# A GLA encoder layer on one core: second-part operands stored by pairs of tiles, half of their blocks kept on chip, and another order of the gate and value products

## The chip, the cores and the metric

The kernel runs on one core of one Trainium2 chip, as one program. The metric is the device time of one execution in microseconds (us). A core has five engines that run their own instruction streams in order: TensorE (PE, matmuls, with a separate weight-load row PEld), VectorE (DVE), ScalarE (ACT), GpSimd (POOL) and SyncE (SP). Here SP only issues DMA transfers. ACT issues some too, between its own instructions.

## The reference, cut to what matters

One layer of an encoder on a sequence of 2048 rows of 1024 numbers in float32: a gated-linear-attention (GLA) mixer, a residual sum, a norm, a convolutional feed-forward part with 2 x 2816 columns up and 1024 down, a second residual sum, and a last norm.

```python
def conv_ffn(h, w_up, conv_w, conv_b, w_down):
    u = causal_dwconv(h @ w_up, conv_w, conv_b)   # three taps along the sequence
    g, val = jnp.split(u, 2, axis=-1)
    return (jax.nn.silu(g) * val) @ w_down

# the layer
h = rmsnorm(x, mix_norm_w)
x = x + gla_mixer(h, w_in, w_gate2, b_gate, norm_w, w_out)
h = rmsnorm(x, ffn_norm_w)
x = x + conv_ffn(h, w_up, conv_w, conv_b, w_down)
return rmsnorm(x, final_norm_w)
```

The change touches the way from the second `rmsnorm` to the products `h @ w_up`, and the order of those products.

## The kernel before, in words

**Products.** Float32 accuracy is made from two float32r numbers, a high part (a cast on ACT, L184) and a low part (a subtraction on DVE, L185); `split` makes both. A product is three matmuls (`mm3p`, L177, L178, L179: high by low, low by high, high by high). Each of the big matrix products is cut into 2 x 2 blocks and made by seven block products p1 to p7 in place of eight (a Strassen-Winograd scheme); their operands are blocks or sums of blocks. p1, p6, p7 and p4 add up in one PSUM bank, p5 and p3 in a second, and p2 has a third.

**Passes.** R, A and B are the projections into the mixer and the scan. Pass Y multiplies by the output projection. When a tile of 128 rows of `x1 = x + y` is complete, `x1_done` (L741) stores it and normalises it (ACT, L747), and `blocks` (L750) transposes it on PE (L756) into two blocks `hb2` of 128 x 512 and stores each to the DRAM scratch `h2f` (L761). There are 16 tiles, so 32 blocks.

**The second-part operands.** For each pair of tiles, `prep_h2` (L764 to L814) loads blocks from `h2f` again (`h2r`, L772), forms the sums that p5, p7, p6 and p4 need (DVE), splits the seven operands into `h2p` (L184, L185), and stores each to the DRAM scratch `hd` with two DMAs of 256 KB (L778). The rows of `hd` are for one half, high or low, of one operand for four pairs, so that one such DMA writes runs of 128 numbers, 512 bytes. `spread` (L816) gives each of these steps a due time on a clock that counts the PE work emitted so far: the first four pairs (sequence half s = 0) during pass Y from Y0 on, a step every Y1 us; the other four pairs (s = 1) during the gate/value products of s = 0, from U0 on, a step every U1 us. In pass Y `h2p` has three buffers, later one.

**Gate and value products, `phase_u(s)`** (L998 to L1147), for each half s of the sequence, 1024 rows. `load_op` (L833) brings the operand of one product on chip with two DMAs of 1 MB, on ACT's queue for s = 0 and on SP's for s = 1. Then come 11 groups g of two column blocks f. A group has 14 jobs (seven products for two blocks), each of 12 matmuls of 128x512. The order of the products is `OPS`: p1, p5, p6, p2, p7, p4, p3. The two raw weight tiles of a block, `ur`, are loaded on SP (L1007) into four buffers; the jobs' weight operands are prepared five jobs ahead (`prep`, L1010): the sums on POOL (L1017, L1020, L1023, and L1026 for p3) into `us` or in place, then the split. The results:
- PSUM bank `ua` collects p1, p6, p7, p4. ACT copies it out as c1, c2, c3 after p1, p6, p7 (`copied`, L1039) and after p4 into the value tile `u` (L1139). The next product into the bank waits for the copy.
- Bank `uc` collects p5 and p3; bank `ub` holds p2.
- `new_u` (L1042) takes one of **three** buffers of tag `u` for the gate (i = 0) or the value (i = 1) of a block and copies two halo columns into it on POOL (L1045). At p2 the gate tile is taken (filled at L1128), at p7 the value tile (filled at L1135, which reads bank `uc`), at p4 the value tile is complete and `conv(1, f)` runs (L1055 on ACT, twice L1057 on DVE), at p3 the gate tile is complete (L1145), `conv(0, f)` runs, and `gated(f)` forms the operand of the down projection; seven operands of 256 KB a group are stored to `ad` by SP (L1068, L1071, L1072, L1084), four of them after sums on POOL (L1078 to L1082).

**Down projection** (L1150 to the end): seven products for two halves, with `ad` and `w_down` as operands.

**What sets the order.** The code emits work in the order above, and a scheduler with a model of the engines puts each engine's instructions in a final order, which the engines keep. DMAs of a core go to eight lanes in turn, and a DMA on a lane is issued only when the DMA before it on that lane has landed: the ninth waits for the first. Where a tile's buffers are used up, the first instruction that writes the next tile waits for the last reader of the oldest.

Of the kernel before, what the change touches and what calls it, by code (L numbers as in the profile page):

```python
# [16 lines left out]
P = 128  # L17
# [3 lines left out]
def f32(ap):  # L21
    return ap.bitcast(F32)
# [3 lines left out]
def hybrid_kernel(  # L26
# [45 lines left out]
    Y0, Y1, U0, U1 = 9.0, 3.6, 20.0, 12.0  # L72
# [13 lines left out]
    OPS = ("p1", "p5", "p6", "p2", "p7", "p4", "p3")  # L86
    PORD = ("p1", "p5", "p6", "p7", "p4", "p2", "p3")
# [642 lines left out]
    def y_open():  # L730
        need(f"scan1_{NTT - 1}", f"scan1_{NTT - 2}")
        sp["bctx"].close()
        sp["actx"].close()
        yp["p"] = p = yp["ctx"].enter_context(tc.tile_pool(name="yp", bufs=1, reuse_waits="tile"))
        spread(range(PAIRS), Y0, Y1, p,
               lambda name: p.tile([P, 512], F32, tag="h2r", name=name, bufs=4),
               lambda name: p.tile([P, 2, 512], F32R, tag="h2p", name=name, bufs=3))
# [12 lines left out]
    def blocks(tt, rws):  # L750

        for k in range(2):
            pt = aux_ps(f"pt_d{tt}_{k}")
            for j in range(HK):
                kt = HK * k + j
                nc.tensor.transpose(pt[:, j * P:(j + 1) * P], rws[:, kt * P:(kt + 1) * P], ident)  # L756
            t = yp["p"].tile([P, 512], F32, tag="hb2", name=f"hb2_{tt}_{k}", bufs=4)
            for j in range(HK):
                kt = HK * k + j
                nc.scalar.activation(t[:, j * P:(j + 1) * P], pt[:, j * P:(j + 1) * P], AF.Identity, scale=nw2[:, kt:kt + 1])  # L760
            nc.sync.dma_start(h2f[tt][k], t)  # L761
        ready.add(f"h2f{tt}")

    def prep_h2(jj, pool, raw, pair):  # L764

        s, j = divmod(jj, PAIRS)
        ts = {}

        def load(n, c, k):
# [10 lines left out]
        sub = nc.vector.tensor_sub  # L780

        def first():
            need(f"h2f{2 * jj}", f"h2f{2 * jj + 1}")
            for n, (c, k) in enumerate(((0, 0), (1, 0), (1, 1))):
                load(n, c, k)

        def p1():
            put("p1", 0)

        def p5():  # L790
            sub(ts[0], ts[1], ts[0])
            put("p5", 0)

        def p7():
            sub(ts[1], ts[2], ts[1])
            put("p7", 1)

        def p3():
            load(1, 0, 1)
            put("p3", 2)  # L800

        def p6():
            sub(ts[0], ts[2], ts[0])
            put("p6", 0)

        def p2():
            put("p2", 1)

        def p4():
            sub(ts[1], ts[1], ts[0])  # L810
            put("p4", 1)
            ready.add(f"h2p{jj}")

        return [first, p1, p5, p7, p3, p6, p2, p4]  # L814
# [18 lines left out]
    def load_op(s, o):  # L833

        t = uh.tile([P, KT, 512], F32R, tag=o, name=f"h_{s}_{o}", bufs=1)
        for i in range(2):
            (nc.scalar if s == 0 else nc.sync).dma_start(f32(t[:, i * HK:(i + 1) * HK, :]), hd[s, o, i])
        hop[o] = (t[:, :HK, :], t[:, HK:, :])
# [159 lines left out]
    def phase_u(s):  # L998
# [11 lines left out]
        def prep(k):  # L1010
# [4 lines left out]
            if o == "p5":  # L1015
                src = sums[f] = out_tile(f"us_{s}_{f}")
                add(src, a21, a22)  # L1017
            elif o == "p6":
                src = sums[f]
                sub(src, src, a11)  # L1020
            elif o == "p7":
                src = a21
                sub(src, a11, a21)  # L1023
            elif o == "p3":
                src = sums.pop(f)
                sub(src, a12, src)  # L1026
            else:
                src = {"p1": a11, "p2": a12, "p4": a22}[o]
# [5 lines left out]
            split(hl[0], hl[1], src)  # L1034
            wops[o, f] = hl
# [54 lines left out]
        for k, (g, o, f) in enumerate(jobs):  # L1090
            if o == "p1" and f == 2 * g and g + 1 < NQ:
                load(g + 1)
            if s == 0 and k == 6:
# [6 lines left out]
                spread(range(PAIRS, 2 * PAIRS), U0, U1, wx_, row_tile,  # L1100
# [11 lines left out]
            pairs = [((wh[:, kt * P:(kt + 1) * P], wl[:, kt * P:(kt + 1) * P]), (hop[o][0][:, kt, :], hop[o][1][:, kt, :])) for kt in range(HK)]  # L1112
# [116 lines left out]
    def d_early(o):  # L1229
# [3 lines left out]
        elif o == "p2":  # L1233
# [147 lines left out]
```

## Time and profile before

| | us |
|---|---|
| median of 3 runs | 2328.84 |
| lowest and highest run | 2320.21, 2340.29 |
| the profiled execution, its own time | 2328.23 |
| span of its trace, first to last instruction | 2326.5 |

The mean granted TensorE clock of the profiled execution is 0.980 of full speed. The trace begins with pass R; pass Y runs from about 750 us to 965 us, the products of s = 0 from about 965 to 1455, those of s = 1 to about 1900, and the down projection to the end. A table by such windows is the way to read this profile, because the stages have different limits. In a row of a waits table, "PE uc L177 <- DVE u L1135" reads: PE's matmul on line 177 into a bank `uc` was idle until DVE's instruction on line 1135 that writes a tile `u`; then the sum in us, the number of times and the longest. In a timeline row the start, the duration, the engine and line, output and inputs; in square brackets the idle time ahead of the instruction and what ended it. "SPq" and "ACTq" are DMA issues of the two engines; a row with x3 is three in a row, from the first issue to the end of the last.

### The profile page before, as it was taken

How to read it: one execution, taken by the hardware profiler on the slowest of the kernel's cores; microseconds unless marked ns; L12 is line 12 of the kernel's file. 1: busy time of each engine (PE TensorE's matmuls, PEld its weight loads, DVE VectorE, ACT ScalarE, POOL GpSimd, SP SyncE). 2: the span in 40 equal slices, each digit the busy share in tenths (PEclk: the TensorE clock that was granted, in tenths of full speed). 3: DMA queues.
4: the chain of work that ended last, by engine and by line, in shares of the span. 5: the costliest groups of instructions: out<-in, count | busy, mean ns of one | idle time of the engine just before them, and what ended most of it. 6: DMA issues, size and time to landing. Idle time of an engine off the chain costs nothing. (4 is left out here: it accounts for less than half of the span.)

```text
span 2326.5 us, 28993 instructions
## 1 busy us (share of the span) xinstructions
PE 2152.4 (93%) x9948; PEld 1746.6 (75%) x9948; DVE 1605.4 (69%) x2175; ACT 1115.9 (48%) x2020; POOL 702.0 (30%) x602
## 2 busy tenths in 40 slices
PE   5999999989997988688898999999999999999998
PEld 4888778877886766566776777877777778888887
DVE  7755787788778555377776777777676786656554
ACT  4554655565555664444444444445444554223243
POOL 1000111111110000245454555464555543134200
PEclk9999999999999999899999999999999999999999
DMA  6545684478556999954444236633323268554443
GB/s 218 191 159 187 203 278 122 124 232 289 166 155 228 304 312 326 350 154 131 138 138 145 77 114 223 223 102 99 106 79 119 75 217 307 180 178 160 135 163 118
DMA packets 344115, 420.14 MB, mean 181 GB/s; under 512 B 22798, under 2 KB 216510, under 8 KB 340384
## 3 DMA queue, kind: packets, MB, share of 16 engines
q1 hardware_dynamic: 313900, 360.35, 47.4%
q10 hardware_dynamic: 30068, 57.95, 7.3%
q8 instruction: 78, 1.28, 0.2%
q14 instruction: 69, 0.57, 0.1%
HBM read 270.89 MB, written 147.32 MB: 180 GB/s over the span
## 5 line engine op out<-in xcount | busy, mean ns | idle before, releaser
L177 PE MATMUL ua<-h_p,uw_p 128*128 128x512 f32 x704 | 283.0, 402 | 24.7 <-ACT c L1039 24.7
L178 PE MATMUL ua<-h_p,uw_p 128*128 128x512 f32 x704 | 281.2, 399 | 0.0
L179 PE MATMUL ua<-h_p,uw_p 128*128 128x512 f32 x704 | 280.8, 399 | 0.0
L1057 DVE SCALAR_TENSOR_TENSOR t<-u,cw,t 128x1024 f32<-128x1024 f32 x176 | 244.6, 1418 | 21.9 <-issue 8.2
L178 PE MATMUL pd_p<-dw_p,da 128*128 128x512 f32 x616 | 239.8, 389 | 0.3 <-DVE da L185 0.3
L177 PE MATMUL pd_p<-dw_p,da 128*128 128x512 f32 x616 | 239.6, 389 | 0.0
L179 PE MATMUL pd_p<-dw_p,da 128*128 128x512 f32 x616 | 239.6, 389 | 0.0
L185 DVE TENSOR_TENSOR da<-da_p,da 128x512 fp32r<-128x512 f32 x154 | 128.9, 891 | 102.9 <-ACT da L184 102.7
L185 DVE TENSOR_TENSOR uw_p<-us,uw_p 128x512 fp32r<-128x512 f32 x132 | 138.4, 1049 | 72.5 <-ACT uw_p L184 71.9
L184 ACT CAST da<-da_p 128x512 fp32r<-128x512 f32 x154 | 85.4, 619 | 204.7 <-PE pd_p L179 154.5
L177 PEld LDWEIGHTS ua<-h_p,uw_p 128*128 128x128 f32 x704 | 135.7, 193 | 58.2 <-ACT c L1039 27.7
L185 DVE TENSOR_TENSOR uw_p<-ur,uw_p 128x512 fp32r<-128x512 f32 x176 | 137.9, 794 | 54.0 <-ACT uw_p L184 52.1
L177 PE MATMUL uc<-h_p,uw_p 128*128 128x512 f32 x352 | 141.6, 402 | 35.1 <-DVE u L1135 35.0
L178 PEld LDWEIGHTS ua<-h_p,uw_p 128*128 128x128 f32 x704 | 135.9, 193 | 30.7 <-DVE uw_p L185 0.4
L179 PEld LDWEIGHTS ua<-h_p,uw_p 128*128 128x128 f32 x704 | 135.5, 193 | 30.8
L184 ACT CAST uw_p<-ur 128x512 fp32r<-128x512 f32 x176 | 107.9, 620 | 72.5 <-PE ub L179 43.8
L178 PE MATMUL uc<-h_p,uw_p 128*128 128x512 f32 x352 | 139.2, 395 | 0.0
L179 PE MATMUL uc<-h_p,uw_p 128*128 128x512 f32 x352 | 139.2, 395 | 0.0
L1039 ACT COPY c<-ua 128x512 f32<-128x512 f32 x132 | 77.1, 584 | 127.2 <-PE ua L179 127.0
L1017 POOL TENSOR_TENSOR us<-ur 128x512 f32<-128x512 f32 x44 | 66.8, 1518 | 234.1 <-DMA ur<-in_ffn_w_up_dram 229.0
L178 PEld LDWEIGHTS pd_p<-dw_p,da 128*128 128x128 f32 x616 | 115.6, 188 | 24.6 <-DVE da L185 0.7
L179 PEld LDWEIGHTS pd_p<-dw_p,da 128*128 128x128 f32 x616 | 115.6, 188 | 24.1
(250 smaller groups left out, 5503.1 us busy)
## 6 DMA issues: line engine op xcount, KB each, us to landing
ur<-in_ffn_w_up_dram SPq DMA_DIRECT2D x84, 512.0 KB, 4.0
da_p<-ad_p SPq DMA_DIRECT2D x154, 256.0 KB, 4.0
hd_p<-h2p_p SPq DMA_DIRECT2D x112, 256.0 KB, 3.9
ad_p<-as_p SPq DMA_DIRECT2D x88, 256.0 KB, 2.0
ad_p<-t SPq DMA_DIRECT2D x66, 256.0 KB, 2.9
x<-in_x_dram SPq DMA_DIRECT2D x32, 512.0 KB, 5.1
ch<-in_ffn_w_down_dram SPq DMA_DIRECT2D x61, 256.0 KB, 4.9
hr_A_p<-h1d_p SPq DMA_DIRECT2D x56, 256.0 KB, 2.8
```

What stands on the lines that cost most here:

```text
L177: nc.tensor.matmul(ps_ap, ah, bl, start=(first and i == 0), stop=False, **kw)
L178: nc.tensor.matmul(ps_ap, al, bh, start=False, stop=False, **kw)
L179: nc.tensor.matmul(ps_ap, ah, bh, start=False, stop=(last and i == len(pairs) - 1), **kw)
L184: nc.scalar.copy(hi, src)
L185: nc.vector.tensor_sub(lo, src, f32(hi))
L1017: add(src, a21, a22)
L1039: nc.scalar.copy(t, pa)
L1057: nc.vector.scalar_tensor_tensor(t, u[:, k:k + TS], cw[:, k, c:c + 1], t, op0=ALU.mult, op1=ALU.add)
```

## The change

1. The blocks of the first eight tiles (s = 0) stay on chip: `hb2` gets ten buffers, and their 16 stores to `h2f` and 16 loads from it go. The blocks of the other eight tiles still go through `h2f`, which has one scratch array per tile now (tag `hb3`, two buffers in place of four).
2. `hd` is kept by pairs: one array [128, 2, 512] per product and pair, with the high and the low part side by side. One store of 512 KB takes the place of two of 256 KB, and it is issued at the next step (`held`), not right behind its split. `load_op` has four DMAs of 512 KB in place of two of 1 MB, and the matmul's moving operand is a view of four runs of 128 numbers, one for each pair.
3. `spread` is one chain of steps that waits until the blocks of a pair are there. Y0, Y1 go from 9.0, 3.6 to 3.0, 2.8, and U1 from 12.0 to 11.0.
4. `OPS` becomes p1, p5, p6, p7, p4, p2, p3, and with it the order of the jobs and of the operand loads. An early load for the down projection hangs on p7 in place of p2.
5. The sum for p3 (POOL) is made right behind the split for p6, and not when p3's weights are prepared.

```diff
-    Y0, Y1, U0, U1 = 9.0, 3.6, 20.0, 12.0
+    Y0, Y1, U0, U1 = 3.0, 2.8, 20.0, 11.0
...
-    OPS = ("p1", "p5", "p6", "p2", "p7", "p4", "p3")
-    PORD = ("p1", "p5", "p6", "p7", "p4", "p2", "p3")
+    OPS = PORD = ("p1", "p5", "p6", "p7", "p4", "p2", "p3")
...
-    h2f = [[scratch([P, 512], f"h2f_{t}_{k}") for k in range(2)] for t in range(NTT)]
+    h2f = {t: scratch([P, 2, 512], f"h2f_{t}") for t in range(TT, NTT)}
...
-    hd = {(s, o, i): scratch([P, HK, 512], f"hd_{s}_{o}_{i}") for s in range(NS) for o in OPS for i in range(2)}
+    hd = {(s, o, j): scratch([P, 2, 512], f"hd_{s}_{o}_{j}") for s in range(NS) for o in OPS for j in range(PAIRS)}
...
-            t = yp["p"].tile([P, 512], F32, tag="hb2", name=f"hb2_{tt}_{k}", bufs=4)
+            t = hb2_tile(f"hb2_{tt}_{k}", tt < TT)
...
-            nc.sync.dma_start(h2f[tt][k], t)
+            if tt < TT:
+                h2[tt, k] = t
+            else:
+                nc.sync.dma_start(h2f[tt][:, k, :], t)
         ready.add(f"h2f{tt}")
 
-    def prep_h2(jj, pool, raw, pair):
+    def hb2_tile(name, kept):
+        return yp["p"].tile([P, 512], F32, tag="hb2" if kept else "hb3", name=name, bufs=10 if kept else 2)
+
+    def prep_h2(jj, raw, pair):
...
         def load(n, c, k):
+            if s == 0:
+                ts[n] = h2.pop((2 * jj + c, k))
+                return
             if n not in ts:
                 ts[n] = raw(f"h2r_{jj}_{n}")
-            nc.sync.dma_start(ts[n], h2f[2 * jj + c][k])
-
-        def put(o, n):
+            nc.sync.dma_start(ts[n], h2f[2 * jj + c][:, k, :])
+
+        def store():
+            while held:
+                o, hl = held.pop()
+                nc.sync.dma_start(hd[s, o, j], f32(hl))
+
+        def step(o, n, x=None, y=None, then=None):
+            store()
+            if x is not None:
+                nc.vector.tensor_sub(ts[n], ts[x], ts[y])
+            if then is not None:
+                then()
             hl = pair(f"h2p_{jj}_{o}")
             split(hl[:, 0, :], hl[:, 1, :], ts[n])
-            for i in range(2):
-                nc.sync.dma_start(hd[s, o, i][:, :, j * P:(j + 1) * P], f32(hl[:, i, :]).rearrange("p (a b) -> p a b", b=P))
+            held.append((o, hl))
...
     def spread(pairs, t0, dt, *how):
-        for n, jj in enumerate(pairs):
+
+        chain_ = []
+        for jj in pairs:
             for i, fn in enumerate(prep_h2(jj, *how)):
-                later_do(t0 + dt * (7 * n + max(0, i - 1)) - (2.0 if i == 0 else 0.0), fn)
+                chain_.append((fn, dt if 0 < i < 8 else 2.0, {f"h2f{2 * jj}", f"h2f{2 * jj + 1}"}))
+
+        def go():
+            fn, us, what = chain_[0]
+            if not ready.issuperset(what):
+                later_do(2.0, go)
+                return
+            chain_.pop(0)
+            fn()
+            if chain_:
+                later_do(us, go)
+
+        later_do(t0, go)
...
-        t = uh.tile([P, KT, 512], F32R, tag=o, name=f"h_{s}_{o}", bufs=1)
-        for i in range(2):
-            (nc.scalar if s == 0 else nc.sync).dma_start(f32(t[:, i * HK:(i + 1) * HK, :]), hd[s, o, i])
-        hop[o] = (t[:, :HK, :], t[:, HK:, :])
+        t = uh.tile([P, 2, PAIRS, 512], F32R, tag=o, name=f"h_{s}_{o}", bufs=1)
+        for j in range(PAIRS):
+            (nc.scalar if s == 0 else nc.sync).dma_start(f32(t[:, :, j, :]), hd[s, o, j])
+        hop[o] = tuple(t[:, i].rearrange("p j (k c) -> p k j c", c=P) for i in range(2))
...
             elif o == "p3":
                 src = sums.pop(f)
-                sub(src, a12, src)
...
             split(hl[0], hl[1], src)
+            if o == "p6":
+                sub(src, a12, src)
             wops[o, f] = hl
...
-        elif o == "p2":
+        elif o == "p7":
             d_load(4)
```

**Where instructions stand now: the `u` tiles (POOL).** In the rows, `u_0_c` is the tile of sequence half 0 and column block c: 4 and 5 are the gates of a group, 26 and 27 its values, 6 and 28 those of the next group. L1045 (L1055 in the change) takes a tile, L1053 (L1063) saves its halo when the first half of `conv` has come. Before:

```order
L1053 COPY halo_500<-u_0_26_10581 128x2
L1020 TENSOR_TENSOR us_0_6_10625<-us_0_6_10625,ur_0_6_10400 128x512
L1020 TENSOR_TENSOR us_0_7_10654<-us_0_7_10654,ur_0_7_10404 128x512
L1026 TENSOR_TENSOR us_0_6_10625<-ur_0_6_10400,us_0_6_10625 128x512
L1045 COPY u_0_27_10601<-halo_500 128x2
L1053 COPY halo_500<-u_0_27_10601 128x2
```

And in the changed kernel:

```order
L1063 COPY halo_504<-u_0_26_10478 128x2
L1063 COPY halo_504<-u_0_27_10502 128x2
L1029 TENSOR_TENSOR us_0_6_10566<-us_0_6_10566,ur_0_6_10342 128x512
L1055 COPY u_0_5_10589<-halo_504 128x2
L1055 COPY u_0_28_10798<-halo_504 128x2
L1029 TENSOR_TENSOR us_0_7_10592<-us_0_7_10592,ur_0_7_10346 128x512
L1063 COPY halo_504<-u_0_4_10563 128x2
L1044 TENSOR_TENSOR us_0_6_10566<-ur_0_6_10342,us_0_6_10566 128x512
```

The fourth tile of the group, the one that can be taken only when the first is free, was the second block's value (27, for p7) and is now the second block's gate (5, for p2). PE's order in a group is now p1, p5, p6, p7 for both blocks, 19 of the 24 matmuls of p2, p4 for both blocks, the last five of p2, p3; before it was p1, p5, p6, p2, p7, p4, p3, with the first block's p1 of the next group begun inside p3.

**The stores of the s = 1 operands in the group (SP).** These are SP's rows in the first groups of s = 0; `ad` and `as` belong to the gated operands, `ur` are raw weight tiles, `hd` the operand stores of `h2p`. Before:

```order
L1084 DMA ad_0_p3_0_404<-as_0_0_p3_10075 128x512
L1084 DMA ad_0_p7_0_382<-as_0_0_p7_10078 128x512
L1007 DMA ur_0_5_10085<-in_ffn_w_up_dram 128x8x128
L1007 DMA ur_0_27_10087<-in_ffn_w_up_dram 128x8x128
L778 DMA hd_1_p2_1_331<-h2p_4_p2_10549 512x1x128
L772 DMA h2r_5_2_10759<-h2f_11_1_277 128x512
L778 DMA hd_1_p4_0_334<-h2p_4_p4_10643 512x1x128
```

And now:

```order
L1094 DMA ad_0_p7_0_375<-as_0_0_p7_10020 128x512
L1016 DMA ur_0_4_10023<-in_ffn_w_up_dram 128x8x128
L1016 DMA ur_0_26_10025<-in_ffn_w_up_dram 128x8x128
L1016 DMA ur_0_5_10027<-in_ffn_w_up_dram 128x8x128
L1016 DMA ur_0_27_10029<-in_ffn_w_up_dram 128x8x128
L785 DMA hd_1_p6_0_322<-h2p_4_p6_10415 128x1024
L785 DMA hd_1_p2_0_334<-h2p_4_p2_10491 128x1024
L780 DMA h2r_5_2_10721<-h2f_11_257 128x512
```

A store of `hd` still stands behind the gated stores of the group and behind raw weight loads, four in a row now where there were two there and two earlier.

**The operand loads of s = 1 (SP).** At the end of s = 0, `h_1_o` is the operand of product o, and the group before it is group 10. Before:

```order
L1084 DMA ad_0_p7_10_392<-as_0_10_p7_13233 128x512
L1007 DMA ur_1_3_13248<-in_ffn_w_up_dram 128x8x128
L1007 DMA ur_1_25_13250<-in_ffn_w_up_dram 128x8x128
L837 DMA h_1_p4_13472<-hd_1_p4_0_334 128x2048
L837 DMA h_1_p4_13472<-hd_1_p4_1_335 128x2048
L837 DMA h_1_p3_13517<-hd_1_p3_0_336 128x2048
```

And now:

```order
L1094 DMA ad_0_p7_10_385<-as_0_10_p7_13151 128x512
L1016 DMA ur_1_2_13162<-in_ffn_w_up_dram 128x8x128
L1016 DMA ur_1_24_13164<-in_ffn_w_up_dram 128x8x128
L1016 DMA ur_1_3_13166<-in_ffn_w_up_dram 128x8x128
L1016 DMA ur_1_25_13168<-in_ffn_w_up_dram 128x8x128
L846 DMA h_1_p4_13357<-hd_1_p4_3_333 128x2x512
L846 DMA h_1_p2_13402<-hd_1_p2_0_334 128x2x512
L846 DMA h_1_p2_13402<-hd_1_p2_1_335 128x2x512
```

Behind the last gated store of group 10 there stood the operands of p4 and p3, and now stand the last quarter of p4, the whole of p2 and that of p3.

More of the change, by code (lines that the diff above doesn't have):

```diff
@@ L734, in y_open @@
         yp["p"] = p = yp["ctx"].enter_context(tc.tile_pool(name="yp", bufs=1, reuse_waits="tile"))
-        spread(range(PAIRS), Y0, Y1, p,
-               lambda name: p.tile([P, 512], F32, tag="h2r", name=name, bufs=4),
+        spread(range(PAIRS), Y0, Y1, None,
                lambda name: p.tile([P, 2, 512], F32R, tag="h2p", name=name, bufs=3))
@@ L790, in p5, with last @@
[L790 to L811, printed above, removed]
-            ready.add(f"h2p{jj}")
-        return [first, p1, p5, p7, p3, p6, p2, p4]
+        def last():
+            store()
+            ready.add(f"h2p{jj}")
@@ L1111, in phase_u @@
             wh, wl = wops.pop((o, f))
[L1112 removed]
+            pairs = [((wh[:, kt * P:(kt + 1) * P], wl[:, kt * P:(kt + 1) * P]), (hop[o][0][:, kt], hop[o][1][:, kt])) for kt in range(HK)]
             if o == "p1":
```

12 lines of the change are left out of this document (7 added, 5 removed).

## The prediction

> **What bounds the kernel now.** I read the busy shares first, then the span in windows by stage, then what PE waited for in each stage, then the chain that ended last inside one stage, and last the timelines of the queues at the places that these name.
>
> ```profile
> PE 2152.4 (93%) x9948; PEld 1746.6 (75%) x9948; DVE 1605.4 (69%) x2175; ACT 1115.9 (48%) x2020; POOL 702.0 (30%) x602
> 750.00:930.00 180.00, 160.75 (x726) 123.69 (x725) 100.32 (x167) 103.26 (x228) 11.73 (x17) 1.00 0.92 309
> 930.00:965.00 35.00, 17.20 (x50) 11.77 (x50) 5.74 (x10) 8.83 (x18) 3.59 (x4) 0.75 1.04 407
> 1005.00:1345.00 340.00, 302.30 (x1234) 241.94 (x1235) 251.60 (x264) 155.75 (x232) 169.74 (x149) 0.94 0.44 130
> 1455.00:1900.00 445.00, 427.07 (x1848) 345.36 (x1847) 329.05 (x339) 215.85 (x317) 230.38 (x173) 1.00 0.41 128
> ```
>
> The window rows give from:to, length, then the busy time (and count) of PE, PEld, DVE, ACT and POOL, the granted clock, the DMA share and GB/s. The kernel is bound by PE nearly everywhere: 93% busy. So a change that removes no matmul can win only where PE idles or runs at a lower clock. Three places show that. Pass Y has 19 us idle in 180 with the DMA engines 92% busy. The change from Y to the products is half idle (17.2 of 35) with the clock at 0.75 and the DMA engines full. And the products of s = 0 take longer than those of s = 1: a group is 14 x 12 = 168 matmuls, so the s = 0 window holds 1234/168 = 7.3 groups, 46 us each, and the s = 1 window 11 groups, 40.5 each. At the full-speed spacing of 0.23 us, which the rows from 1243.63 further down show, a group would take 38 to 39 us. The down projection (417.88 of 426 busy) has nothing to give, and the passes before Y are in the same order before and after.
>
> ```profile
> PE uc L177 <- DVE u L1135: 35.0, 20, 3.0
> PE ua L177 <- ACT c L1039: 24.4, 6, 4.9
> PE uc L177 <- DVE u L1135: 14.0, 7, 3.0
> PE uc L177 <- DVE u L1135: 21.1, 13, 2.3
> ```
>
> The first row is of the whole span, the second and third of 965 to 1345, the fourth of 1345 to 1900. So two waits make the products slow: p3 of the second block waits for L1135 to free bank `uc` in nearly every group, and p4 waits for the ACT copy c3 in s = 0 alone, some 4 us each time. The chain inside one group of s = 0 says what is behind both (start, length, what):
>
> ```profile
> 1220.33 1.11 DVE uw_p L185
> ...
> 1222.48 5.53 DMA hd_p<-h2p_p
> ...
> 1228.60 0.59 ACT c L1039
> 1229.23 0.79 PE ua L177
> ...
> 1234.69 0.59 ACT u L1139
> ...
> 1235.80 1.15 ACT t L1055
> 1236.97 2.01 DVE t L1057
> ...
> 1242.47 0.61 DVE u L1135
> 1243.13 0.50 PE uc L177
> 1243.63 0.23 PE uc L178
> 1243.86 0.23 PE uc L179
> ```
>
> Read from the end: p3 (1243.13) waits for L1135 of the second block, which writes the group's fourth `u` tile; its buffer comes free only through L1139, L1055 and both L1057 of the first block, that is after p4. In the first half of the piece p4 (1229.23) waits for c3 (1228.60), and that follows the DMA of an operand store, which SP could issue only at 1222.48, behind a raw weight load, which waited for the split (1220.33) that freed its buffer. Why ACT waits for a store, and why SP is late, the two queues show:
>
> ```profile
> 1228.08 0.62 ACT L184 CAST h2p_p<-h2r 128x512 fp32r<-128x512 f32 x1 [8.53 <-DMA hd_p<-h2p_p]
> 1214.10 7.12 SPq L1084 DMA_DIRECT2D ad_p<-as_p  x4
> 1221.31 1.11 SPq L1007 DMA_DIRECT2D ur<-in_ffn_w_up_dram  x2
> ```
>
> `h2p` has one buffer in these groups, so the next cast waits for the last operand's store, and c3 is queued behind that cast on ACT.
>
> **The change part by part**, against the profiled execution's own 2328.23 us (0.6 below the median of the runs).
>
> *New order of the products (part 4).* p7 now stands ahead of p2, so the fourth `u` tile of a group is the second block's gate, filled by p2 from bank `ub`, which PE needs again only in the next group. L1135's two tiles are the first and second block's values, free early. All of the wait goes: **-35.0**. A tile still waits, but 24 matmuls of p3 and 96 of the next group stand between it and PE. The next late thing would be DVE, 251.6/7.3 = 34 us busy a group, which fits into 39. Bounds: -35 and, if the wait only moves, 0.
>
> *Early sum for p3, and the order (parts 4, 5) at c3.* In the new order the rows on ACT are the same: the cast of an operand ahead of c3, the store on SP behind the gated stores and now four raw loads. But 19 matmuls of p2 stand between p7 and p4 (19 x 0.227 = 4.3 us more for c3), and the raw buffers come free sooner. Against that, two more raw loads stand ahead of the store (1.11 us for two, and their wait for the split). In the piece above the copy was 4.95 us late; 4.3 of slack less about 1.5 to 2.5 for what is new ahead of the store leaves about 2 of a mean 24.4/6 = 4.1. Of 24.4 I take off **-11**; bounds: -24.4 (all covered) and +10 (the store later by what the slack gives, twice in three groups).
>
> *The clock.* After the stalls of s = 0 PE runs at a lower clock for some time: 0.06 x 340 = 20 us in that window.
>
> ```profile
> 1007.18 0.50 PE L177 MATMUL uc<-h_p,uw_p 128*128 128x512 f32 x1 [2.96 <-DVE u L1135]
> 1149.07 0.79 PE L177 MATMUL uc<-h_p,uw_p 128*128 128x512 f32 x1 [2.73 <-DVE u L1135]
> 1229.23 0.79 PE L177 MATMUL ua<-h_p,uw_p 128*128 128x512 f32 x1 [4.95 <-ACT c L1039]
> ```
>
> A gap of 4.95 and one of 2.73 are followed by slow matmuls (0.79), one of 2.96 is not (0.50). Check of the whole: 7.3 groups at 38.2 are 280 us, and 340 - 280 = 60; the two waits (38 in 965 to 1345) and the clock (20) give 58. With gaps of about 2 us left at p4, I take half of the clock loss back: **-9**; bounds 0 and -20. The Trainium skill, "TensorE: Matmul & The Clock Gate", section "HAM oscillation", puts the border at idle gaps above about 3.4 us. By that the whole loss would come back once the gaps at p4 fall to 2, and the sum would be 11 lower; the row after 2.73 us speaks against so sharp a border.
>
> *Blocks kept, stores by pairs, in pass Y (parts 1, 2, 3).*
>
> ```profile
> PE mp_Y L177 <- ACT h_Y_p L184: 11.9, 7, 5.6
> PE pt_d L756 <- ACT h L747: 10.2, 4, 7.8
> q1 hardware_dynamic: 45118, 49.44, 88.8%
> hd_p<-h2p_p SPq DMA_DIRECT2D x56, 256.0 KB, 5.0
> h2f<-hb SPq DMA_DIRECT2D x26, 256.0 KB, 4.2
> ```
>
> The first two rows are of 750 to 965, the others of 765 to 930. Of the traffic, 16 stores and 16 loads of 256 KB go (8 of 49 MB), and 56 operand stores become 28 of twice the size in longer runs. Of the two waits, 5.6 and 7.8 belong to the change to the products, so (11.9 - 5.6) + (10.2 - 7.8) = 9 is the most that DMA relief gives in Y. I take **-5**; bounds 0 and -9. DVE and ACT work in Y is the same, so the rest of the idle time stays.
>
> *Operand loads at the change from Y to the products (part 2).* They are 28 DMAs of 512 KB on ACT's queue in place of 14 of 1 MB.
>
> ```profile
> h_p<-hd_p ACTq DMA_DIRECT2D x14, 1024.0 KB, 9.6
> 948.01 7.17 ACTq L837 DMA_DIRECT2D h_p<-hd_p  x4
> 948.47 0.79 PE L177 MATMUL mp_Y<-w_Y_p,h_Y_p 128*128 128x512 f32 x1 [5.59 <-ACT h_Y_p L184]
> 962.03 1.97 PE L756 MATMUL pt_d<-ident,h 128*128 128x128 f32 x8 [7.77 <-ACT h L747]
> ```
>
> Four loads held ACT for 7.17 us, because a DMA waits for the one eight before it; PE's two long waits here are for ACT instructions queued behind such loads. With halves, the eight lanes hold half the bytes, so ACT stays for one operand more, 2 MB at 407 GB/s: 5 us, against lighter store traffic. I take **+5**; bounds -5 (the stores end sooner and both waits shrink) and +12 (both waits grow by 5 to 6). A rule that speaks against smaller DMAs is in the Trainium skill, "DMA: Bandwidth & Descriptors", beside its bandwidth figures: at least 1 MiB each for 75% of peak. The fit on "SBUF — State Buffer", section "The DMA setup-cost knee", 2 us and bytes by 436 GB/s, gives as an estimate 0.8 us more for each megabyte cut in two, 11 us for 14, and the sum would be 6 higher. The window's 407 GB/s with eight in flight says that fixed costs overlap here.
>
> *Operand loads from s = 0 to s = 1.* They stand on SP in the order p1, p5, p6, p7, p4, p2, p3.
>
> ```profile
> 1458.56 0.39 PE L177 MATMUL uc<-h_p,uw_p 128*128 128x512 f32 x1
> 1467.84 4.64 SPq L1084 DMA_DIRECT2D ad_p<-as_p  x4
> ```
>
> The first row is in p5 of the first group of s = 1; its p1, 24 matmuls of 0.23, puts the group's start at about 1453. Before, only p4 and p3 stood behind the gated stores of group 10; now p2 does. It would be issued after 1467.84 + 4.64 = 1472.5 (stores), 2.2 (four raw loads, 1.11 for two) and their wait for free buffers, so at about 1477, and land after 4 to 9 us (half of 9.6 to all of it), at 1481 to 1486; p2's turn on PE is 96 matmuls after the start, at 1475. So **+6**; bounds 0 (the gated stores are earlier as the waits go) and +12.
>
> *The rest.* One load later for the down projection and the store held for a step cost nothing: PE is 98% busy there, with loads well ahead. The 16 us of POOL sums are the same in number.
>
> **The sum**: 2328.2 - 35 - 11 - 9 - 5 + 5 + 6 = 2279, so about **2280 us**.
>
> **The rivals.**
> *The store keeps the pace of s = 0.* The slack at c3 is eaten by SP's later store; then p4's wait and the clock stay: 2328 - 35 - 5 + 5 + 6 = 2299. For it speaks that ACT's order is as before and the store stands behind more.
> *The store is covered.* Both waits and all of the clock loss go, and the two changes between stages cost nothing: 2328 - 35 - 24 - 20 - 9 = 2240. For it speaks 4.3 us of slack against a mean wait of 4.1; against it the raw loads ahead of the store.
> *The change doesn't do what it says.* The `u` wait moves to another tile (DVE, in order, holds L1135 of the next block behind a p2 fill that waits for its buffer): 2279 + 35 = 2314. Against it: L1135 comes ahead of the second p2 fill on DVE.
> *Slower: the split operand.* Every matmul of both halves now reads its moving operand in four runs of 128. The first row below counts 704 on one of three lines for four of the seven products, so there are 704 x 7/4 x 3 = 3696.
>
> ```profile
> L177 PE MATMUL ua<-h_p,uw_p 128*128 128x512 f32 x704 | 283.0, 402 | 24.7 <-ACT c L1039 24.7
> L1039 ACT COPY c<-ua 128x512 f32<-128x512 f32 x132 | 77.1, 584 | 127.2 <-PE ua L179 127.0
> L1139 ACT COPY u<-ua 128x512 f32<-128x512 f32 x44 | 25.9, 589 | 71.7 <-DVE u L1135 40.4 <-PE ua L179 27.9 <-POOL u L1045 3.4
> ```
>
> If that costs 49/3696 = 13 ns each (of 0.23 us), the gain is gone; at 20 ns the kernel is 1% slower, at 25 ns it takes 2279 + 92 = 2371. No row shows PE reading so; the nearest, ACT writing four runs (589 ns) against one (584), says 5 ns, which would be +18 at worst.
>
> **How the numbers follow.** My forecast has 0.52 (2260 to 2298 for itself), the covered store 0.16, the kept pace 0.17, the moved wait 0.08, the split operand 0.07. The range leaves out the split operand and some of the extreme ends: 2238 to 2318. About 1% (23 us) is what a measurement of this kernel tells from no change. Faster by more: 0.52 + 0.16 + 0.10 of the kept pace = 0.78. Within: 0.07 of the kept pace and 0.07 of the moved wait = 0.14. Slower: 0.08.
>
> **What would show it.** PE's waits for L1135 (its new line) should be gone in both halves; if another wait of 1 to 3 us stands at p3 in each group, the first term is wrong. PE's wait for c3 should be about half, and the granted clock of s = 0 about 0.97. In Y the DMA share should fall from 0.92; between Y and the products ACT's issues should hold the last normalisation longer; p2 of the first s = 1 group should wait 5 to 8 us for its load. Matmul spacing should stay at 0.23; if it doesn't, the forecast falls as a whole. A group of s = 1 should take 38.5, one of s = 0 about 41.

## The result: slower by about 1%

The changed kernel takes 2355.18 us (median of 4 runs, 2348.30 to 2357.74) against 2327.95 for the kernel before (median of 4 runs): a ratio of 1.0107, 95% interval 1.0058 to 1.0157. The forecast was 2280 us, in 2238 to 2318. The profiled execution took 2357.74 us, with a span of 2356.0, which is 29.5 us more than the 2326.5 of before.

The page of the changed kernel, its busy shares and the clock in 40 slices:

```profile
PE 2157.6 (92%) x9948; PEld 1758.3 (75%) x9948; DVE 1655.0 (70%) x2175; ACT 1106.7 (47%) x2020; POOL 700.4 (30%) x602
PEclk9999999999999998999999999899999999999999
```

Its windows, with the columns of the prediction (from:to, length, busy of PE, PEld, DVE, ACT and POOL with counts, clock, DMA share, GB/s):

```profile
750.00:930.00 180.00, 164.88 (x756) 132.22 (x755) 103.12 (x173) 106.82 (x239) 11.30 (x17) 0.96 0.87 308
930.00:965.00 35.00, 23.14 (x86) 18.06 (x84) 8.37 (x15) 16.54 (x36) 9.50 (x11) 0.71 0.86 312
1005.00:1345.00 340.00, 299.95 (x1230) 241.03 (x1229) 258.76 (x251) 145.77 (x223) 165.65 (x143) 0.94 0.42 129
1455.00:1900.00 445.00, 408.35 (x1743) 329.85 (x1742) 332.96 (x312) 194.74 (x293) 226.46 (x168) 0.97 0.37 109
```

Pass Y got further in the same time (756 and 86 matmuls where 726 and 50 ran before). The products of s = 0 are no faster, and those of s = 1, at clock 1.00 before, fell from 1848 to 1743 matmuls in the same 445 us. To split the 29.5 us I take the first matmul of p5 in each half and the last matmul of the products. For the changed kernel these rows are

```profile
956.35 0.39 PE L176 MATMUL uc<-h_p,uw_p 128*128 128x512 f32 x1
1457.07 0.39 PE L176 MATMUL uc<-h_p,uw_p 128*128 128x512 f32 x1
1928.61 0.40 PE L178 MATMUL uc<-h_p,uw_p 128*128 128x512 f32 x1
```

and for the kernel before they stand at 971.46, 1458.56 and 1899.87. So the stages up to the products gained 15.1 us, s = 0 lost 13.6 (500.7 in place of 487.1), s = 1 lost 30.2 (471.5 in place of 441.3), and the rest lost 0.8: together 29.5.

What PE waited for in the changed kernel (the first two rows are of the whole span, the third of 965 to 1445, the fourth of 1445 to 1925; L176 and L1049 are L177 and L1039 of before):

```profile
PE ua L176 <- ACT c L1049: 80.3, 21, 6.5
PE ub L176 <- DMA h_p<-hd_p: 14.4, 1, 14.4
PE ua L176 <- ACT c L1049: 52.7, 11, 6.5
PE ua L176 <- ACT c L1049: 27.5, 10, 5.3
```

The 35.0 us of waiting for the value tile at p3 are gone, all of them, as forecast. But PE's waits for ACT's copies out of bank `ua`, 24.7 us before, are 80.3. All three copies c1, c2 and c3 have line 1049; the place of each wait in PE's order tells which it is. 70.5 us are p4 waiting for c3, in 9 groups of s = 0 and 10 of s = 1, where before it was 24.4 us in 6 groups of s = 0 and 0.3 us in one of s = 1. The other 9.8 us are p7 waiting for c2, in two groups of s = 0, like this one, which stands behind 24 matmuls of p6:

```profile
1155.05 0.72 PE L176 MATMUL ua<-h_p,uw_p 128*128 128x512 f32 x1 [4.91 <-ACT c L1049]
```

And p2 of the first s = 1 group waits 14.4 us for its operand. These waits account for the loss. PE's waits from 965 to 1445 us grew from 41.4 us, those for the value tile among them, to 52.7, and from 1445 to 1925 from 18.3 to 41.9. Matmuls 0.3 to 0.6 us apart in place of 0.23, which show the lower clock, cost an estimated 3 us more in s = 0 and 7 more in s = 1.

One group of s = 1 shows how c3 comes to be late. First SP in the changed kernel, then SP at the same place in a group of the kernel before (`ad` rows are the gated stores, `ur` rows the raw weight loads):

```profile
1647.11 5.43 SPq L1094 DMA_DIRECT2D ad_p<-as_p  x4
1652.62 3.94 SPq L1016 DMA_DIRECT2D ur<-in_ffn_w_up_dram  x4
```

```profile
1619.33 0.37 SPq L1007 DMA_DIRECT2D ur<-in_ffn_w_up_dram  x1
1620.45 0.53 SPq L1068 DMA_DIRECT2D ad_p<-t  x1
1622.37 0.37 SPq L1007 DMA_DIRECT2D ur<-in_ffn_w_up_dram  x1
1625.81 0.52 SPq L1071 DMA_DIRECT2D ad_p<-t  x1
1626.38 0.63 SPq L1072 DMA_DIRECT2D ad_p<-t  x1
1629.06 6.69 SPq L1084 DMA_DIRECT2D ad_p<-as_p  x4
1635.85 1.14 SPq L1007 DMA_DIRECT2D ur<-in_ffn_w_up_dram  x2
```

Before, the two raw loads of the next group's first block were out ahead of most of the gated stores. Now all four stand behind them. Then DVE and ACT in that group of the changed kernel, while PE ran p2's first 19 matmuls from 1655.13 on and then stood:

```profile
1656.72 0.62 ACT L183 CAST uw_p<-ur 128x512 fp32r<-128x512 f32 x1 [3.35 <-DMA ur<-in_ffn_w_up_dram]
1657.37 0.69 DVE L184 TENSOR_TENSOR uw_p<-ur,uw_p 128x512 fp32r<-128x512 f32 x1 [3.28 <-ACT uw_p L183]
1658.06 0.69 DVE L1138 TENSOR_TENSOR u<-ub,c 128x512 f32<-128x512 f32 x1
1660.34 0.62 ACT L183 CAST uw_p<-ur 128x512 fp32r<-128x512 f32 x1 [3.00 <-DMA ur<-in_ffn_w_up_dram]
1660.86 0.58 ACT L1049 COPY c<-ua 128x512 f32<-128x512 f32 x1
```

The copy c3 (1660.86) is queued on ACT behind the casts of both blocks' p1 of the *next* group, and these wait for the late raw loads. PE goes on at 1661.50. That these casts stand ahead of c3 has a reason. Buffers of tag `cp` are four, and c1 and c2 of a group's two blocks fill them. c3 of the first block needs a buffer again, and the first to come free is c1's, which is read when p2 is evicted (L1138, the 1658.06 row). Since p2 comes after p7 in the new order, c3 must now wait for p2's product and its eviction. In the order of the instructions with their waits, ACT and DVE read (8 and 9 are the blocks of a group, 10 and 11 those of the next; the DVE count that line 1521 waits for is the one that line 1621 brings):

```
1519 L183 CAST uw_1_10_p1_14580<-ur_1_10_14406 128x512 [waits DVE_49,DMAHW3_49,PE_49,Activation_49]
1520 L183 CAST uw_1_11_p1_14600<-ur_1_11_14410 128x512 [waits DMAHW5_49,DVE_49,PE_49]
1521 L1049 COPY c3_1_8_14535<-ua_1_8_14419 128x512 [waits DVE_49]
...
1620 L184 TENSOR_TENSOR uw_1_10_p1_14580<-ur_1_10_14406,uw_1_10_p1_14580 128x512 [waits DMAHW3_49,Activation_49]
1621 L1138 TENSOR_TENSOR u_1_8_14616<-ub_1_8_14603,c1_1_8_14432 128x4x128 [waits PE_49]
```

In s = 0 one thing more stands ahead of c3 on ACT, as it did before: the cast of an s = 1 operand, which waits for the one buffer of `h2p`. One such group of the changed kernel, with the c3 row at the end:

```profile
1117.08 0.62 ACT L183 CAST h2p_p<-h2r 128x512 fp32r<-128x512 f32 x1 [6.26 <-DMA hd_p<-h2p_p]
1117.61 0.61 ACT L183 CAST uw_p<-ur 128x512 fp32r<-128x512 f32 x1
1118.13 0.58 ACT L1049 COPY c<-ua 128x512 f32<-128x512 f32 x1
```

So two suspects stand: the raw buffers that come free late (A), and the four copy buffers that push c3 behind the casts (D). The experiments tell them apart, and them from the rest of the change. The kernel before was run beside each batch (medians 2330.26, 2330.07 and 2326.76); ratios are against these.

### The profile page after: what moved, and what is told of

Same layout as the page of the kernel before. It is cut to its first block, busy times and chain, and to the rows that moved or that the text cites. A ratio compares the mean times of both kernels' runs of the same rounds, so it can differ in the third digit from the quotient of the medians.

```text
span 2356.0 us, 28886 instructions
## 1 busy us (share of the span) xinstructions
PE 2157.6 (92%) x9948; PEld 1758.3 (75%) x9948; DVE 1655.0 (70%) x2175; ACT 1106.7 (47%) x2020; POOL 700.4 (30%) x602
## 5 line engine op out<-in xcount | busy, mean ns | idle before, releaser
L176 PE MATMUL ua<-h_p,uw_p 128*128 128x512 f32 x704 | 290.4, 413 | 82.3 <-ACT c L1049 80.3
L177 PE MATMUL ua<-h_p,uw_p 128*128 128x512 f32 x704 | 286.4, 407 | 0.0
L178 PE MATMUL ua<-h_p,uw_p 128*128 128x512 f32 x704 | 285.2, 405 | 0.0
L184 DVE TENSOR_TENSOR uw_p<-ur,uw_p 128x512 fp32r<-128x512 f32 x176 | 200.7, 1174 | 106.3 <-ACT uw_p L183 106.2
L1067 DVE SCALAR_TENSOR_TENSOR t<-u,cw,t 128x1024 f32<-128x1024 f32 x176 | 264.2, 1532 | 14.7 <-ACT t L1065 14.2
L176 PE MATMUL pd_p<-dw_p,da 128*128 128x512 f32 x616 | 239.6, 389 | 0.0
L177 PE MATMUL pd_p<-dw_p,da 128*128 128x512 f32 x616 | 239.6, 389 | 0.0
L176 PEld LDWEIGHTS ua<-h_p,uw_p 128*128 128x128 f32 x704 | 138.8, 197 | 123.7 <-ACT c L1049 90.3
L178 PEld LDWEIGHTS ua<-h_p,uw_p 128*128 128x128 f32 x704 | 138.7, 197 | 32.1
L177 PEld LDWEIGHTS ua<-h_p,uw_p 128*128 128x128 f32 x704 | 139.2, 198 | 31.1 <-DVE uw_p L184 0.4
L184 DVE TENSOR_TENSOR uw_p<-us,uw_p 128x512 fp32r<-128x512 f32 x132 | 111.0, 846 | 66.4 <-ACT uw_p L183 65.7
L178 PE MATMUL uc<-h_p,uw_p 128*128 128x512 f32 x352 | 138.1, 392 | 0.0
L176 PE MATMUL uc<-h_p,uw_p 128*128 128x512 f32 x352 | 138.1, 392 | 0.0
L177 PE MATMUL uc<-h_p,uw_p 128*128 128x512 f32 x352 | 138.0, 392 | 0.0
L177 PEld LDWEIGHTS pd_p<-dw_p,da 128*128 128x128 f32 x616 | 115.6, 188 | 24.1
L178 PEld LDWEIGHTS pd_p<-dw_p,da 128*128 128x128 f32 x616 | 115.6, 188 | 24.1
L176 PEld LDWEIGHTS pd_p<-dw_p,da 128*128 128x128 f32 x616 | 115.6, 188 | 23.9
L183 ACT CAST uw_p<-us 128x512 fp32r<-128x512 f32 x132 | 81.7, 619 | 110.3 <-POOL us L1029 69.6
```

The source lines that it names most:

```text
L176: nc.tensor.matmul(ps_ap, ah, bl, start=(first and i == 0), stop=False, **kw)
L177: nc.tensor.matmul(ps_ap, al, bh, start=False, stop=False, **kw)
L178: nc.tensor.matmul(ps_ap, ah, bh, start=False, stop=(last and i == len(pairs) - 1), **kw)
L183: nc.scalar.copy(hi, src)
L184: nc.vector.tensor_sub(lo, src, f32(hi))
L1067: nc.vector.scalar_tensor_tensor(t, u[:, k:k + TS], cw[:, k, c:c + 1], t, op0=ALU.mult, op1=ALU.add)
```

## The experiments

**The order undone, all else kept.**

```diff
-    OPS = PORD = ("p1", "p5", "p6", "p7", "p4", "p2", "p3")
+    OPS = ("p1", "p5", "p6", "p2", "p7", "p4", "p3")
+    PORD = ("p1", "p5", "p6", "p7", "p4", "p2", "p3")
...
-        elif o == "p7":
+        elif o == "p2":
```

> The changed kernel with the old order of the products alone (p1, p5, p6, p2, p7, p4, p3; the early sum, the pair storage and the kept blocks stay). Theory A (the new order holds the first raw weight buffer of a block until the split for p2, the last but one; the next group's raw loads then stand behind the gated stores on SP, the casts for the next p1 wait for them on ACT, and the copy c3 is queued behind these casts): PE's wait for c3 in s = 1 falls from 27.5 us to under 3, the wait for the value tile at p3 comes back with about 20 us in s = 1, the 14.4 us wait for p2's operand goes, and what is left of the change is its gain ahead of the products, about 12 us: 2305 to 2325 us. Theory B (the operand by pairs costs: 28 loads of 512 KB, and four runs per matmul): within 10 us of the changed kernel's 2355. Theory C (the early sum costs, on POOL and DVE): also above 2340.

It took 2318.30 us, ratio 0.9957 (0.9935 to 0.9978). Its waits over the whole span:

```profile
PE uc L177 <- DVE u L1146: 36.5, 21, 2.9
PE ua L177 <- ACT c L1050: 32.8, 7, 6.8
```

The value-tile wait is back (18.4 us of it in s = 1), c3's is gone from s = 1 (0.4 us there) and the operand wait is gone. Parts 1, 2, 3 and 5 together gain about 12 us, 0.4 to 0.5%, in the range that A gave; the loss is the order's.

**The order and the early sum alone, on the kernel before.** Diff: parts 4 and 5 as in the change.

> The kernel before with the new order of the products and the early sum alone (storage and loads as before). Theory A: PE's wait for c3 is 25 to 30 us in s = 1 and about 50 in s = 0, the value-tile wait at p3 is gone, the operand of p2 comes late at the start of s = 1, and nothing is gained ahead of the products: 2345 to 2370 us, slower than before by 1 to 2%. Theory B: the order alone gains what the removed wait was worth: 2290 to 2310. Theory C: slower as well; the next run tells it from A.

2370.59 us, ratio 1.0181 (1.0160 to 1.0202), at the upper end of A's range. The first row below is the wait for the copies over the whole span (62.7 us of it for c3, 15.9 for c2), the second p2's operand, which here comes as two loads of 1 MB:

```profile
PE ua L176 <- ACT c L1039: 78.6, 21, 8.5
PE ub L176 <- DMA h_p<-hd_p: 13.8, 1, 13.8
```

The order, with the early sum, costs 40 us on this storage. The storage by pairs has no part in it: B falls.

**The early sum undone.**

```diff
                 src = sums.pop(f)
+                sub(src, a12, src)
...
-            if o == "p6":
-                sub(src, a12, src)
```

> The changed kernel with the sum for p3 made late again, when p3's weights are prepared. Theory A: the first raw buffer's last reader is the split for p2 either way, so the time stays within 6 us of the changed kernel's 2355. Theory C (the early sum costs): 2340 or less.

2355.49 us, ratio 1.0100 (1.0074 to 1.0127), the same as the change. The early sum is worth nothing that shows either way: with it and without it, SP's next raw loads wait for the splits of p2 and p4. C falls.

**p2 ahead of p4.** This moves the last reader of each block's first raw buffer (p2) two jobs earlier and leaves p7 ahead of p2.

```diff
-    OPS = PORD = ("p1", "p5", "p6", "p7", "p4", "p2", "p3")
+    OPS = ("p1", "p5", "p6", "p7", "p2", "p4", "p3")
+    PORD = ("p1", "p5", "p6", "p7", "p4", "p2", "p3")
```

> The changed kernel with the order p1, p5, p6, p7, p2, p4, p3: the fourth value or gate tile is still the second block's gate, but the first raw buffer of each block is freed by the split for p2 ahead of that for p4, and its next load stands ahead of the gated stores again. Theory A: PE's wait for c3 in s = 1 falls from 27.5 us to under 10, the value-tile wait at p3 stays under 5, and the operand of p2 for s = 1 is loaded ahead of p4's, so that its wait of 14.4 us shrinks or goes: 2300 to 2330 us, faster than before by up to 1%. Theory B: within 10 us of 2355.

2303.15 us, ratio 0.9888 (0.9871 to 0.9904), faster than before. The size of the gain is as A has it, but 15.3 us of c3's wait are left in s = 1 where A gave under 10. In s = 0 PE's wait for the copies is 37.7 us, some 26 of it for c3. The wait for p2's operand shrank from 14.4 to 8.3 us. So the raw loads are not all of it. How much of the gain is theirs this run can't say: the order also brings p2's eviction, which frees c1's buffer, ahead of p4, and so eases D as well.

**c3 in another ring of buffers**, that of the gated sums (tag `as`, four buffers), the changed kernel otherwise untouched:

```diff
-                u3 = copied(f"c3_{s}_{f}", a)
+                u3 = pools["us"].tile([P, 512], F32, tag="as", name=f"c3_{s}_{f}", bufs=4)
+                nc.scalar.copy(u3, a)
```

> The changed kernel with the copy c3 in buffers of tag as in place of tag cp; nothing else. Theory D (the four buffers of tag cp hold c1 and c2 of both blocks; c1 is read at p2, which now comes after p7, so c3 of the first block can't be written until p2's product has been read, and for that the copy has its place on ACT behind the casts of the next group's p1): c3 now stands ahead of these casts, PE's wait for c3 in s = 1 falls from 27.5 us to under 6, in s = 0 from 52.7 to under 30, although the raw loads come as late as before: 2285 to 2315 us. Theory A alone (only the late raw buffers matter): c3's wait stays above 15 us in s = 1 and the time within 12 us of 2355.

2279.12 us, ratio 0.9789 (0.9765 to 0.9812): 6 us below the range that D gave, so D was right in kind and too small. In the windows (one in s = 0, one in s = 1) the products of s = 1 are what they can be:

```profile
1005.00:1345.00 340.00, 318.29 (x1353) 257.24 (x1352) 279.07 (x277) 162.04 (x248) 189.18 (x160) 0.98 0.43 137
1455.00:1830.00 375.00, 375.00 (x1636) 306.79 (x1635) 295.11 (x289) 181.53 (x271) 209.73 (x151) 1.00 0.36 106
```

PE is busy 375.00 of 375.00 us at the full clock. One group of s = 1 on ACT, where L1143 is now the copy c3 and the last row is a cast of the next group's p1:

```profile
1590.64 0.59 ACT L1143 COPY c<-ua 128x512 f32<-128x512 f32 x1 [1.73 <-issue]
1591.12 0.62 ACT L183 CAST uw_p<-us 128x512 fp32r<-128x512 f32 x1
1593.36 0.59 ACT L1143 COPY c<-ua 128x512 f32<-128x512 f32 x1 [1.61 <-issue]
1593.84 0.62 ACT L183 CAST uw_p<-ur 128x512 fp32r<-128x512 f32 x1
```

What is left in s = 0 and at the start of s = 1:

```profile
PE ua L176 <- ACT c L1049: 24.1, 11, 3.8
PE ua L176 <- issue: 10.0, 1, 10.0
```

L1049 is now c1 and c2 alone: nearly all of the 24.1 us is p6 waiting for c1, and what holds c1 up in s = 0 I didn't take apart; DVE, which I had named as the next late thing, is busy 279 of 340 us there. The second row is the first matmul of p4 in s = 1 ("issue" means that the profile names no releaser; by its place it is the wait for p4's operand). PE waits for c3 nowhere any more. Out of the shared ring c3 stands ahead of the next group's casts on ACT, PE's order in a group becomes p7, p4, p2 as `OPS` has it, and the raw loads, three of four still behind the gated stores, hold up no copy. D stands.

**Both remedies at once** (p2 ahead of p4, c3 in buffers of tag `as`).

> The order p1, p5, p6, p7, p2, p4, p3 with the copy c3 in buffers of tag as. Theory D: c3's wait goes here too (under 6 us in s = 1, where the order alone left 15.3): 2280 to 2303 us, faster than the order alone. Theory A: nothing left to gain, 2300 to 2310.

2286.89 us, ratio 0.9820 (0.9792 to 0.9848). PE waits for c3 in neither half, against 15.3 us in s = 1 with the order alone, as D expects (1.2 us in s = 1 are for c2); but p2 waits 11.6 us for its operand at the start of s = 1. With the ring out of the way, moving p2 gains nothing more.

**Loads of 1 MB.** The scratch holds two pairs per array, and one DMA loads two pairs.

```diff
-    hd = {(s, o, j): scratch([P, 2, 512], f"hd_{s}_{o}_{j}") for s in range(NS) for o in OPS for j in range(PAIRS)}
+    hd = {(s, o, j): scratch([P, 2, 2, 512], f"hd_{s}_{o}_{j}") for s in range(NS) for o in OPS for j in range(PAIRS // 2)}
...
-        for j in range(PAIRS):
-            (nc.scalar if s == 0 else nc.sync).dma_start(f32(t[:, :, j, :]), hd[s, o, j])
+        for j in range(PAIRS // 2):
+            (nc.scalar if s == 0 else nc.sync).dma_start(f32(t[:, :, 2 * j:2 * j + 2, :]), hd[s, o, j])
```

> The changed kernel with its operands loaded by two DMAs of 1 MB in place of four of 512 KB, the layout on chip and in runs of 2 KB as changed. If the size of the loads is what made the change from Y to the products shorter (the first p5 of the products starts 11.7 us earlier than before), that gain goes: first p5 at 965 us or later, the time up by 5 to 12. If it costs, as predicted: earlier by about 5 us. If the kept blocks and the stores by pairs did it: no change, within 4 us of 2355. The wait for p2's operand at the start of s = 1 stays at 12 to 16 us if its place on SP's queue decides, and halves if the size does.

2350.14 us, ratio 1.0099 (1.0069 to 1.0129), against the changed kernel's 1.0107: not to be told apart. Its first p5 stands at 945.9, 10 us earlier, but that is one trace: in the other runs with kept blocks, all with loads of 512 KB, it stands between 944.6 and 956.4. The median is 5 us lower, so at most some 5 us hang on the size, and that is not shown. p2's wait at the start of s = 1 is 13.2 us: its place in the queue makes it, not the size.

**The blocks through DRAM again** (`hb2` in four buffers, all 16 tiles stored to and loaded from `h2f`).

```diff
-            if tt < TT:
-                h2[tt, k] = t
-            else:
-                nc.sync.dma_start(h2f[tt][:, k, :], t)
+            nc.sync.dma_start(h2f[tt][:, k, :], t)
...
-            if s == 0:
-                ts[n] = h2.pop((2 * jj + c, k))
-                return
```

> The changed kernel with the blocks of the first eight tiles stored and loaded through DRAM again, as those of the other eight; pair storage, order and due times as changed. If the kept blocks are what gained the 11.7 us ahead of the products, the first p5 starts at about 970 us and the time rises by 8 to 15 to 2363 to 2370; if the stores by pairs did it, the time stays within 4 us of 2355.

2370.28 us, ratio 1.0176 (1.0154 to 1.0199): 15 us above the change. Its first p5 stands here:

```profile
970.36 0.39 PE L176 MATMUL uc<-h_p,uw_p 128*128 128x512 f32 x1
```

It is near the 971.46 of before, and all the traces bear this out: without kept blocks the first p5 stands at 963.2 to 971.5 (four kernels), with them at 944.6 to 956.4 (eight). So the kept blocks made the gain ahead of the products, some 15 us. The stores by pairs and the new due times gain nothing that shows: this run and the one with the order alone on the old storage, 2370.28 and 2370.59 us, are the same.

**The remedy on the kernel before** (the order, the early sum, c3 in buffers of tag `as`; storage and loads as before).

> The kernel before with the new order, the early sum and the copy c3 in buffers of tag as, its storage and loads as before. Theory D: the order without the shared ring of copy buffers gains on this kernel what it does on the changed one, so this is the changed kernel with c3 in its own buffers (2279) plus the 12 to 15 us that the kept blocks are worth: 2288 to 2298 us. If the order needs the pair storage to gain: 2310 or more.

2303.21 us, ratio 0.9900 (0.9880 to 0.9921): a miss by 5 us at the upper end. With c3 in other buffers the order gains without the pair storage. How much of this gain the old order would have got from c3's other buffers alone, no run shows. The two kernels, this one and the changed one with c3 moved, differ by 24 us in the medians, and not by the 15 of the kept blocks alone. In the profiled executions (spans 2294.2 and 2275.0) 13 of 19 us stand ahead of the products; the rest is spread over both halves, and I didn't take it apart.

**The late operands on another queue**, with c3 in buffers of tag `as`.

```diff
-            (nc.scalar if s == 0 else nc.sync).dma_start(f32(t[:, :, j, :]), hd[s, o, j])
+            (nc.scalar if s == 0 or o in ("p4", "p2", "p3") else nc.sync).dma_start(f32(t[:, :, j, :]), hd[s, o, j])
```

> The changed kernel with c3 in its own buffers, and the operands of p4, p2 and p3 for s = 1 loaded on ACT's queue, past the gated stores and raw loads on SP. If their place on SP's queue is what makes PE wait 10 us at p4 of the first group of s = 1, that wait falls to under 3 us: 2266 to 2274. If ACT is held by the lanes and its copies come late in place of it: 2279 or more.

2280.03 us, ratio 0.9794 (0.9779 to 0.9808), no better than 2279.12. The wait of 10.0 us at p4 is gone, but one of 3.5 us stands now at p6 of the same group, and PE's waits for ACT's copies in s = 1 rose from 2.1 to 6.8 us:

```profile
PE ua L176 <- ACT c L1049: 6.8, 7, 3.0
PE ua L176 <- issue: 3.5, 1, 3.5
```

The waits moved from p4's operand to p6 and to ACT's copies c1 and c2, whose queue now has the loads too.

## Why the prediction was wrong, point by point

*The value-tile wait, -35.0: right.* It is gone in the changed kernel and in every run with p7 ahead of p2, and back (36.5) where the order is undone.

*c3, -11: wrong in sign, and the step that failed.* It measured +45.8 (p4's wait for c3, 24.7 to 70.5), and 9.8 more at p7 for c2, which no term had. Two sentences failed. "In the new order the rows on ACT are the same" is not so: two casts of the next group's p1 stand ahead of c3. And "19 matmuls of p2 stand between p7 and p4 (19 x 0.227 = 4.3 us more for c3)" took PE's new order as slack. The order of the instructions showed p2 ahead of p4 although `OPS` has p4 ahead of p2, and that was the sign of a dependency: p4 waits for c3, c3 for a copy buffer, the buffer for p2's eviction. With c3 in other buffers p4 stands ahead of p2 again. I had counted the `u` tiles' three buffers and not the copies' four. "The raw buffers come free sooner" was wrong too: p2 became the last reader of each block's first raw buffer, and the run without the early sum shows that the sum frees nothing. With c3 in other buffers, s = 1 takes what I had forecast for it, 38.5 us a group, and the kernel 2279 us for a forecast of 2280. That the two numbers meet is partly luck, for that is another kernel than the one forecast, and the terms below don't meet.

*The clock, -9: wrong in sign.* The clock of s = 0 stayed at 0.94 in its window, and that of s = 1 fell from 1.00 to 0.97. That would be 13 us of 445, but part of it lies in the waits themselves: by the distances of the matmuls the lower clock cost some 7 us more in s = 1 and 3 more in s = 0. The new waits were long enough for it (last section).

*Pass Y, -5, with 0 and -9 as ends, and the change to the products, +5: mis-sized.* Together they came to -15.1. The run with the blocks through DRAM shows that the kept blocks did it (15 us). The cap of 9 came from the two largest rows of waits, for ACT's `h_Y_p` and `h`; from 750 us to the first p5 they fell only from 22.1 to 19.7, while the waits for DVE there, which the cap left out, fell from 13.3 to 5.2. What made the rest is not shown. The cost of smaller loads was put at 5 us by the rows; with loads of 1 MB the median is 5 us lower, which is inside the uncertainty. The Trainium skill, "SBUF — State Buffer", section "The DMA setup-cost knee", has a fit of 2 us and bytes by 436 GB/s. The 0.8 us for each megabyte cut in two, 11 us for 14, don't follow from it: an estimate by that fit is 2 us each, 28 us, for loads one after the other. No run shows either cost.

*From s = 0 to s = 1, +6: right in mechanism, mis-sized.* p2's operand came 14.4 us late, above the upper end of 12; its place in SP's queue made the wait, as forecast. SP's rows at that place in the changed kernel:

```profile
1465.60 5.42 SPq L1094 DMA_DIRECT2D ad_p<-as_p  x4
1471.12 4.80 SPq L1016 DMA_DIRECT2D ur<-in_ffn_w_up_dram  x4
1475.97 7.38 SPq L846 DMA_DIRECT2D h_p<-hd_p  x9
```

The stores ended at 1471.0, near the 1472.5 that I had reckoned, but issuing the four raw loads took 4.8 us and not 2.2, and the operand landed after 1486, my late end: PE went on at 1488.19.

*The split operand, the rival on the other side: no cost.* The mean distance from one matmul to the next into the same bank, over the pairs less than 0.26 us apart, is 0.2294 us before and 0.2297 after from 965 to 1445 us (1621 and 1583 pairs), and 0.2296 and 0.2297 from 1445 to 1900. So it costs at most 0.3 ns each, 1 us in 3696, against the 13 ns at which it would have decided. That the kernel is slower, to which I gave 0.08, came by none of my rivals: nearest was the store that keeps its pace, and no rival had c3 wait in s = 1 at all.

## What to carry to other kernels

When an order is changed to take pressure off one ring of buffers, go through every ring that the same steps use: the new order shortens the life of some tiles and lengthens that of others, and the price comes where the lengthened one (here c1) shares its ring with a copy on the critical path. Where a scheduler's order differs from the order in the code, ask which wait made it differ before counting the difference as slack. A copy that frees a PSUM bank should not be queued behind casts that wait for the next group's loads; moving it to another ring, with no more room, turned a loss of 1.1% into a gain of 2.1%.

## What the runs showed of the hardware

The same subtraction on DVE (the low part of a split) took 0.69 us alone and about 1.5 us beside POOL's sums. In the changed kernel, five in a row while POOL formed the gated sums (1645.40 to 1652.2), and one at another time:

```profile
1645.24 7.50 DVE L184 TENSOR_TENSOR uw_p<-ur,uw_p 128x512 fp32r<-128x512 f32 x5
1643.50 0.69 DVE L184 TENSOR_TENSOR uw_p<-ur,uw_p 128x512 fp32r<-128x512 f32 x1
```

The mean of these splits in s = 1 rose from 777 ns before to 1247 ns. The next raw loads wait for some of them, but what that costs no run shows. The Trainium skill, "SBUF — State Buffer", section "Who interferes with whom", has it that a DVE instruction with two inputs in SBUF contends with a GpSimd instruction that reads SBUF; these rows agree.

The clock after a gap of PE: in the products of the changed kernel, no gap of 1.84 to 2.89 us was followed by matmuls at half speed, and each of 3.32 us or more was, for 3 to 6 us. That is near the 3.4 us of the Trainium skill, "TensorE: Matmul & The Clock Gate", section "HAM oscillation". In the kernel before, gaps of 2.11, 2.17 and 2.73 us in s = 0 were followed by half speed too, so it isn't sharp. And the slow matmuls can begin a microsecond after the gap, as here:

```profile
1703.67 0.51 PE L176 MATMUL ua<-h_p,uw_p 128*128 128x512 f32 x1 [3.32 <-ACT c L1049]
...
1704.46 0.40 PE L176 MATMUL ua<-h_p,uw_p 128*128 128x512 f32 x1
1704.69 0.60 PE L177 MATMUL ua<-h_p,uw_p 128*128 128x512 f32 x1
1705.09 0.63 PE L178 MATMUL ua<-h_p,uw_p 128*128 128x512 f32 x1
```

The spacing is 0.23 us up to 1704.69, and 0.40 us and more from there. The first matmul behind a gap, by which the prediction judged, doesn't tell.
